# Low weight parts on GpSimd: one subtraction per row block instead of one per weight tile

## The chip, the cores and the metric

The kernel runs on one core of one Trainium2 chip. The metric is the device time of one execution in microseconds (us). Before the change three runs took 1737.58, 1738.07 and 1731.9 us; their median is 1737.58 us.

The engines are named as the profile names them: PE is the matrix engine and PEld its weight load, DVE the vector engine, ACT the scalar engine, POOL the GpSimd engine, and SP the queue that issues the kernel's DMAs. Each engine takes its own instructions in order. Where one needs another's result, it waits on a semaphore.

## What is computed

The reference is one inference step of a two-layer decoder trunk, for a prompt of 1024 tokens and 8 samples of 4 tokens (1056 columns in all), at model width 1024. Layer 0 is sliding-window attention, layer 1 a gated DeltaNet. Cut to what matters here:

```python
for layer in range(DEPTH):                      # DEPTH = 2
    hp, gp = modulate(xp, c_prompt, norm_g[layer], w_mod[layer], b_mod[layer])
    hs, gs = modulate(xs, c_sample, norm_g[layer], w_mod[layer], b_mod[layer])
    if layer % N_MIXERS == 0:
        op, kp, vp = swa_branch(hp, swa_w_in[j], swa_sinks[j], swa_w_out[j])
        ...
    else:
        op, cp, sp = gdn_branch(hp, conv0, s0, gdn_w_in[j], gdn_conv_w[j], ...)
        ...
    xp = xp + gp * op
    xs = xs + gs * osm
y_prompt = rms_norm(xp, final_norm_g)
```

Both branches begin with `h @ w_in`. In layer 0 `w_in` is 1024 x 2560, in layer 1 it is 1024 x 6176. Everything is float32. These input projections are the work that the change touches.

## The kernel before

**The products.** PE's fast float32 form (`fp32r`) keeps fewer bits than float32. So each operand is kept as a high part, which is the value rounded to that form, and a low part, which is what the rounding left. A product is the sum of three: high x high, high x low and low x high. For the activations these are `hhi`, `hlo` (layer 0) and `h2hi`, `h2lo` (layer 1), in eight row blocks of 128 rows of the model width. For the weights they are `wh` and `wl`.

**A weight tile.** A projection makes 128 output rows for all 1056 columns. Its weights, 1024 x 128, come in two halves. Each half is one tile of 128 partitions x 4 row blocks x 128 columns, loaded by `load_raw` (line 441) into one of four `wr` buffers. `split_w` (line 449) then makes the two parts: ACT casts the whole half into `wh` (line 456), and POOL subtracts that from the raw half into `wl` (line 457), 128 x 512 elements in one instruction. There are three `wh` and three `wl` buffers.

**Who calls it.** The first four halves (lines 716 and 722) and two more (line 749) belong to the opening part of layer 0, in which PE runs `first_half` (line 693) between the modulation's products. `vproj` (line 861) splits four tiles of 2 row blocks x 256 columns (`wvh`, `wvl`). `projector` (line 575) serves 15 projections of layer 0 and 47 of layer 1, two halves each. `first_weights` (line 1433) splits two halves for the first key projection of layer 1 (`kw0l`, `kw1l`), and `decays` (line 1522) two small tiles of 4 row blocks x 32 columns (`wab`).

**A projection in time.** `project` (line 548) walks the column groups 0:384, 384:768 and 768:1056. In each it walks the eight row blocks, with three matmuls for each: `wh` with the high activations, `wh` with the low ones, `wl` with the high ones. The eight row blocks of one group are eight ticks, a projection is 24 ticks. The first row block of the second half is needed at the fifth tick. While projection i runs, the job `ahead` (line 597) issues the loads of projection i+2 and the two splits of projection i+1, at ticks 2 and 20 (`SP`).

**What sets the order.** From line 1287 on, all instructions go through `Core`, a planner that runs while the program is written. `Core.issued` (line 111) charges each instruction a start and a length and keeps `free[engine]` and, for each tile, when it was written and last used. Between any two matmuls of a projection, `stages` (line 496) lets the waiting jobs (attention blocks, the DeltaNet's chains, gating, convolution taps, sample columns) issue what the planner holds to be ready: `ready`, `soon` and `idle` (lines 520 to 527) compare those times. `project` calls `until(ready(hi, lo))` at the first row block of each half, for the whole tiles `hi` and `lo`. The order found so is then fixed on every engine. The planner's charge on POOL is its element count per partition `n` by a rate and a fixed part:

```python
"gpsimd": (420, 0.02 if n >= 256 else 0.14)
```

An instruction that writes a tile which an instruction of the same engine last used starts at least 0.1 us after that one (`after`, line 161).

**What else POOL does.** In layer 1 it also computes the sample columns' convolution (`tp`, `us`, from `XS`), clears and fills the diagonal blocks of the triangular inverse (`UZ`, `Xd`, the latter from `Xc`, which a DMA brings), and computes the reciprocal square roots of the output norm (`rst`, `rsw`, `fo`; ACT scales `vo` with `fo`). DVE at the same time runs the convolution taps (`vT`, `kT`, `qT`), the decay blocks (`DP`) and the row-by-row inversion (`tmp`, `X`).

Of the kernel before, what the change touches and what calls it, by code (L numbers as in the profile page):

```python
# [191 lines left out]
def f(ap):  # L192
    return ap.bitcast(F32)
# [26 lines left out]
def body(tc, I, O, cst_ap, dbg=None):  # L220
    nc = tc.nc
# [227 lines left out]
    def split_w(raw, alloc=None):  # L449
        nk, ncol = raw.shape[1:]  # L450
        if alloc is None:
            hi = wq.tile([P, nk, ncol], F32R, tag="wh", name="wh", bufs=3)
            lo = wq.tile([P, nk, ncol], F32R, tag="wl", name="wl", bufs=3)
        else:
            hi, lo = alloc()
        last_split[:] = [nc.scalar.copy(hi, raw)]
        nc.gpsimd.tensor_sub(lo, raw, f(hi))
        return hi, lo

    def load_w(pieces, rows_ap, ncol, nk=4, alloc=None):  # L460

        return split_w(load_raw(pieces, rows_ap, ncol, nk), alloc)
# [112 lines left out]
    def projector(plan):  # L575
# [8 lines left out]
        def w_split(i, q):  # L584
            if i < len(plan):
                halves_.setdefault(i, []).append(split_w(raws[i][q]))
# [134 lines left out]
    with tc.issue_after(hi_.ins):  # L721
        fws[1] = [split_w(raw) for raw in raws]
# [39 lines left out]
    if True:  # L762
# [469 lines left out]
        for t in range(NB + 1):  # L1232
# [3 lines left out]
            for k in range(KD):  # L1236
                hi, lo = wv[k // 2]
# [49 lines left out]
        nc = Core(tc)  # L1287
# [23 lines left out]
    if True:  # L1311
# [124 lines left out]
        for i, t in enumerate(turned_):  # L1436
# [7 lines left out]
            for kk, hf in order if i < NB else sorted(order, key=lambda o: o[::-1]):  # L1444
                if True:
# [8 lines left out]
                    for k in range(4 * kk, 4 * kk + 4):  # L1454
# [3 lines left out]
                        hi, lo = whi[k][:, ns], wlo[k][:, ns]  # L1458
# [1221 lines left out]
    nc = nc.nc  # L2680
# [36 lines left out]
```

## Time and profile before

| | us |
|---|---|
| median of three runs | 1737.58 |
| profiled execution, its own time | 1730.22 |
| its span, first to last instruction | 1728.1 |
| PE busy | 1628.6 |
| PEld busy | 1432.1 |
| DVE busy | 1207.9 |
| ACT busy | 862.0 |
| POOL busy | 603.2 |

A row of a group of instructions gives: line, engine, operation, the tiles as out<-in, the shapes as partitions x elements, the count, then busy time in us, the mean of one in ns, and the idle time of the engine just before them with what ended it. Line 89 is the planner's recording call, so most instructions carry it, and the tile names tell them apart. A row of the view of stretches gives: the stretch and its length, then for each engine its busy time and (in brackets) its instructions, then the granted share of PE's clock, the DMA share and the DMA rate. A row of the timeline gives: start, length, engine, line, operation, tiles, shapes, count.

### The profile page before, as it was taken

How to read it: one execution, taken by the hardware profiler on the slowest of the kernel's cores; microseconds unless marked ns; L12 is line 12 of the kernel's file. 1: busy time of each engine (PE TensorE's matmuls, PEld its weight loads, DVE VectorE, ACT ScalarE, POOL GpSimd, SP SyncE). 2: the span in 40 equal slices, each digit the busy share in tenths (PEclk: the TensorE clock that was granted, in tenths of full speed). 3: DMA queues.
4: the chain of work that ended last, by engine and by line, in shares of the span. 5: the costliest groups of instructions: out<-in, count | busy, mean ns of one | idle time of the engine just before them, and what ended most of it. 6: DMA issues, size and time to landing. Idle time of an engine off the chain costs nothing. (4 is left out here: it accounts for less than half of the span.)

```text
span 1728.1 us, 31800 instructions
## 1 busy us (share of the span) xinstructions
PE 1628.6 (94%) x10666; PEld 1432.1 (83%) x10666; DVE 1207.9 (70%) x3538; ACT 862.0 (50%) x2514; POOL 603.2 (35%) x1170
## 2 busy tenths in 40 slices
PE   6999999998999899799999999999999998989897
PEld 5988888986777889689989999899998996667685
DVE  4526675564565678877887789778798876357677
ACT  4625555444334565256554665654756555332332
POOL 2601111112122334354443544545345454332322
PEclk9999999999999999899999999999999999999999
DMA  9542121233233232132412323224232137764785
GB/s 330 152 134 72 52 58 50 55 98 106 85 130 103 81 79 67 53 88 56 126 36 75 102 59 107 69 77 112 50 107 62 46 97 211 228 200 130 233 277 184
DMA packets 281573, 191.77 MB, mean 111 GB/s; under 512 B 98362, under 2 KB 253882, under 8 KB 281379
## 3 DMA queue, kind: packets, MB, share of 16 engines
q1 hardware_dynamic: 281410, 189.75, 38.1%
q8 instruction: 84, 1.38, 0.3%
q14 instruction: 79, 0.64, 0.1%
HBM read 144.68 MB, written 47.04 MB: 111 GB/s over the span
## 5 line engine op out<-in xcount | busy, mean ns | idle before, releaser
L89 PE MATMUL ps_pj<-h2hi,wl 128*128 128x384 f32 (+1 forms) x1128 | 380.4, 337 | 2.2 <-POOL wl L89 2.2
L89 PE MATMUL ps_pj<-h2hi,wh 128*128 128x384 f32 (+1 forms) x1128 | 378.3, 335 | 2.1 <-ACT wh L89 2.1
L89 PE MATMUL ps_pj<-h2lo,wh 128*128 128x384 f32 (+1 forms) x1128 | 379.4, 336 | 0.0
L89 POOL TENSOR_TENSOR wl<-wr,wh 128x512 fp32r<-128x512 f32 x122 | 164.4, 1348 | 517.5 <-ACT wh L89 432.9
L89 PEld LDWEIGHTS ps_pj<-h2hi,wl 128*128 128x128 f32 x1128 | 213.6, 189 | 6.2 <-POOL wl L89 3.1
L89 PEld LDWEIGHTS ps_pj<-h2hi,wh 128*128 128x128 f32 x1128 | 213.5, 189 | 4.3 <-ACT wh L89 2.4
L89 PEld LDWEIGHTS ps_pj<-h2lo,wh 128*128 128x128 f32 x1128 | 213.5, 189 | 3.2
L89 POOL TENSOR_TENSOR xt<-xt,y 128x512 f32<-128x512 f32 (+1 forms) x48 | 63.9, 1333 | 188.2 <-DVE y L89 165.1
L89 PE MATMUL ps_pj<-hlo,wh 128*128 128x384 f32 (+1 forms) x360 | 119.0, 331 | 0.0
L89 PE MATMUL ps_pj<-hhi,wh 128*128 128x384 f32 (+1 forms) x360 | 118.4, 329 | 0.0
L89 PE MATMUL ps_pj<-hhi,wl 128*128 128x384 f32 (+1 forms) x360 | 117.9, 328 | 0.0
L89 DVE SCALAR_TENSOR_TENSOR vT<-XR,cT,vT 128x384 f32<-128x384 f32 (+1 forms) x144 | 93.0, 658 | 29.0 <-ACT vT L89 27.1
L89 DVE TENSOR_TENSOR tmp<-X 64x31 f32<-64x31 f32 (+15 forms) x248 | 94.0, 379 | 10.4 <-POOL X L89 7.1
L89 DVE TENSOR_TENSOR X<-X,tmp 64x31 f32<-64x31 f32 (+15 forms) x248 | 94.6, 381 | 8.5
L89 ACT CAST wh<-wr 128x512 fp32r<-128x512 f32 x122 | 75.1, 616 | 16.4 <-PE ps_pj L89 12.0
L89 PEld LDWEIGHTS ps_pj<-hlo,wh 128*128 128x128 f32 x360 | 67.7, 188 | 11.2 <-issue 11.1
L89 ACT COPY XR<-ps_pj 128x384 f32<-128x384 f32 (+1 forms) x96 | 43.0, 448 | 55.9 <-PE ps_pj L89 55.7
L89 POOL TENSOR_TENSOR Xd<-Xc,cst 32x128 f32<-32x128 f32 x128 | 63.4, 495 | 21.2 <-DMA Xc<-Xdd 10.4
L89 PEld LDWEIGHTS ps_pj<-hhi,wh 128*128 128x128 f32 x360 | 67.7, 188 | 2.7 <-issue 2.7
L89 ACT ACTIVATE prob<-prob,nm 128x256 f32<-128x256 f32 (+1 forms) x128 | 62.2, 489 | 14.8 <-DVE nm L89 14.6
L89 PEld LDWEIGHTS ps_pj<-hhi,wl 128*128 128x128 f32 x360 | 67.7, 188 | 2.1 <-issue 2.1
L89 ACT ACTIVATE vo<-vo,fo 128x128 f32<-128x128 f32 x128 | 42.3, 392 | 54.0 <-POOL fo L89 54.0
(574 smaller groups left out, 4218.1 us busy)
## 6 DMA issues: line engine op xcount, KB each, us to landing
wr<-in_gdn_w_in SPq DMA_DIRECT2D x96, 256.0 KB
S<-in_state_gdn_s SPq DMA_DIRECT2D x40, 256.0 KB
xt<-in_x_prompt SPq DMA_DIRECT2D x16, 512.0 KB
wm<-in_w_mod SPq DMA_DIRECT2D x16, 512.0 KB
wr<-in_swa_w_in SPq DMA_DIRECT2D x64, 128.0 KB
wmod<-in_w_mod SPq DMA_DIRECT2D x32, 256.0 KB
wm<-in_w_mod SPq DMA_DIRECT2D x32, 256.0 KB
DP<-gcr SPq DMA_DIRECT2D x64, 128.0 KB
```

Source lines behind the costliest of these rows:

```text
L89: inst = fn(*args, **kwargs)
```

## The change

`split_w` issues the subtraction once for each row block: four instructions of 128 x 128 for a half tile, two of 128 x 256 for each of the four tiles of `vproj`, four of 128 x 32 for each of the two tiles of `decays`. The cast on ACT stays one instruction. What is computed is the same.

```diff
         last_split[:] = [nc.scalar.copy(hi, raw)]
-        nc.gpsimd.tensor_sub(lo, raw, f(hi))
+
+        for k in range(nk):
+            nc.gpsimd.tensor_sub(lo[:, k], raw[:, k], f(hi[:, k]))
         return hi, lo
```

## The prediction

> **What bounds the kernel now.** I read the page first, then the stretches, then what PE waited for, then the timeline around the subtractions.
>
> ```profile
> span 1728.1 us, 31800 instructions
> PE 1628.6 (94%) x10666; PEld 1432.1 (83%) x10666; DVE 1207.9 (70%) x3538; ACT 862.0 (50%) x2514; POOL 603.2 (35%) x1170
> ...
> L89 POOL TENSOR_TENSOR wl<-wr,wh 128x512 fp32r<-128x512 f32 x122 | 164.4, 1348 | 517.5 <-ACT wh L89 432.9
> ```
> ```profile
> 110.00:410.00 300.00, 293.48 (x2146) 255.18 (x2146) 188.49 (x691) 158.21 (x515) 42.63 (x36) 1.00 0.26 71
> 410.00:555.00 145.00, 137.72 (x690) 106.23 (x691) 77.78 (x236) 53.87 (x123) 34.80 (x30) 0.98 0.37 115
> 555.00:1000.00 445.00, 414.52 (x2859) 388.37 (x2857) 351.25 (x971) 240.98 (x718) 185.93 (x443) 0.98 0.29 75
> 1000.00:1443.00 443.00, 433.74 (x3083) 407.75 (x3083) 364.43 (x996) 258.58 (x821) 213.79 (x512) 1.00 0.31 83
> ```
>
> PE sets the time: it is busy in 94% of the span. From 110 to 1443 us, where nearly all of the changed subtractions lie, it is idle for 6.5 + 7.3 + 30.5 + 9.3 = 53.6 us (each stretch less its first busy time). POOL is half empty there (its busy time is the last one in the row), and it has idled 517.5 us ahead of the `wl` subtractions alone, nearly always for ACT's cast. DVE is second, at 80% in the last two rows.
>
> What PE loses to the low parts is small:
>
> ```profile
> PE ps_mi L89 <- DVE us L89: 6.7, 8, 1.6
> ...
> PE ps_lg L89 <- DVE UZ L89: 4.9, 7, 2.0
> ...
> PE ps_mi L89 <- DVE S L89: 3.5, 4, 2.1
> ...
> PE ps_pj L89 <- POOL wl L89: 2.2, 2, 1.5
> ```
> ```profile
> PEld ps_lg L89 <- POOL Xd L89: 5.2, 3, 2.3
> ...
> PEld ps_pj L89 <- POOL wl L89: 3.1, 3, 1.8
> ```
>
> The weight load waited three times for `wl`, 3.1 us together; the matmuls' 2.2 us are two of the same places.
>
> **The change part by part.** *POOL's own time.* There are 122 + 8 subtractions into `wl` and two into `kw0l`, `kw1l` that become four each. No 128 x 128 subtraction into `wl` exists in the trace, but the same operation on such a shape does, and a series with 128 elements on 32 partitions:
>
> ```profile
> L89 POOL TENSOR_TENSOR Xd<-Xc,cst 32x128 f32<-32x128 f32 x128 | 63.4, 495 | 21.2 <-DMA Xc<-Xdd 10.4 <-DVE UZ L89 2.0 <-ACT th L89 1.4
> ...
> L89 POOL TENSOR_TENSOR us<-us,tp 128x32 f32<-128x32 f32 x96 | 30.1, 313 | 8.0
> ...
> L89 POOL TENSOR_TENSOR wab<-wab,wab 128x128 fp32r<-128x128 f32 x2 | 0.9, 457 | 0.4 <-ACT wab L89 0.4
> ```
>
> Four at 457 ns are 1828 ns against 1348, so +0.48 us a half tile. The bounds: four at 450 ns (0.9 us busy for two) are +0.45, four at 495 ns (a mean that holds some disturbed ones) are +0.63. Over 132 halves that is 63 us more on POOL, 59 to 83. The two `wab` tiles go from one of 457 to four of 313 ns, +0.8 us each; the four `wvl` tiles only halve, between nothing and +0.48 each. All of this lies in POOL's idle time unless something is queued behind it. If nothing covered it, the price would be the whole 63 us.
>
> *What is queued behind it.* The samples' convolution, `Xd`, `UZ` and the chain of `rst` to `fo` sit behind a subtraction on POOL, and SP's load into the freed `wr` buffer waits for the subtraction, with other DMAs behind that load. The chain of work that ended last passes over a `wl` subtraction four times:
>
> ```profile
> 1038.56 1.83 POOL wl L89
> ...
> 1075.49 1.28 POOL wl L89
> 1077.27 3.22 DMA Xc<-Xdd
> ...
> 1256.56 1.30 POOL wl L89
> 1262.36 1.25 POOL wl L89
> ```
>
> At 1075.49 it is just this case: the `Xc` transfer left SP's queue after `wl` was done, and `Xd` then waits for it. I charge the four steps of the chain, 4 x 0.48 = +1.9 us. The lower bound is nothing, since another chain of almost the same length may take over; the upper bound is treated with the rivals.
>
> *The head start.* The first row block is finished after 0.46 us instead of 1.35. One of the three stalls shows what that is worth:
>
> ```profile
> 857.07 0.34 PE L89 MATMUL ps_pj<-h2lo,wh 128*128 128x384 f32 x1
> 858.90 0.45 PE L89 MATMUL ps_pj<-h2hi,wl 128*128 128x384 f32 x1 [1.50 <-POOL wl L89]
> ```
> ```profile
> 857.43 0.20 POOL L89 TENSOR_TENSOR fo<-rst,rsw 128x4 f32<-128x4 f32 x1
> 857.58 1.27 POOL L89 TENSOR_TENSOR wl<-wr,wh 128x512 fp32r<-128x512 f32 x1
> ```
>
> The subtraction stood behind the chain to `fo`, and the first matmul on `wl` began 0.05 us after its end. With pieces it could begin at about 858.1, 0.8 us earlier. It then uses one row block every three matmuls, and POOL makes one every 0.46 us, so the later pieces keep up:
>
> ```profile
> 911.24 0.34 PE L89 MATMUL ps_pj<-h2lo,wh 128*128 128x384 f32 x1
> 911.41 0.34 PE L89 MATMUL ps_pj<-h2hi,wl 128*128 128x384 f32 x1
> 911.59 0.34 PE L89 MATMUL ps_pj<-h2hi,wh 128*128 128x384 f32 x1
> ```
>
> Matmuls start 0.17 us apart, three in 0.52 us. Three stalls at up to 0.89 us give −2.7 us; the bounds are 0 and −3.1, for a stall can't give more than it has. That PE waits for pieces singly shows in the opening part, where it read block 2 of `hlo` while POOL was still writing block 3 of the same tile:
>
> ```profile
> 48.88 0.34 PE L702 MATMUL ps_pj<-hlo,wh 128*128 128x384 f32 x1
> ```
> ```profile
> 46.81 2.59 POOL L675 TENSOR_TENSOR hlo<-fu,hhi 128x1024 fp32r<-128x1024 f32 x1 [0.73 <-ACT hhi L674]
> ```
>
> *PE's added waits.* Three more matmuls of each half wait on POOL. Where the wait was long fulfilled, as at 911.41 (the first use of a half whose subtraction, below, ended at 909.16), the matmuls keep their 0.17 us, so I charge nothing; 10 ns on each of some 390 would be 3.9 us, my upper bound.
>
> ```profile
> 907.87 1.29 POOL L89 TENSOR_TENSOR wl<-wr,wh 128x512 fp32r<-128x512 f32 x1 [6.07 <-ACT wh L89]
> ```
>
> *DVE beside POOL.* While a subtraction runs, some DVE operations stretch:
>
> ```profile
> 1036.66 0.37 DVE L89 TENSOR_TENSOR X<-X,tmp 64x207 f32<-64x207 f32 x1
> ...
> 1039.16 1.48 DVE L89 TENSOR_TENSOR tmp<-X 64x231 f32<-64x231 f32 x1
> ```
> ```profile
> 697.59 0.51 DVE L89 TENSOR_TENSOR tmp<-X 64x192 f32<-64x192 f32 x1
> ```
> ```profile
> 695.71 2.72 POOL L89 TENSOR_TENSOR Xd<-Xc,cst 32x128 f32<-32x128 f32 x5
> ```
>
> Alone such an operation takes 0.37 us; beside the `wl` of 1038.56 it took 1.48; beside a series of short POOL instructions, which is what the change makes, 0.51, one after another, while POOL kept a pace of 0.54. A dense series would cost DVE 4 x 0.14 = 0.56 us a half against 1.1 at once. DVE's gain is then up to half a us for each half that meets such operations, up to 132 x 0.55 = 73 us of DVE time if all did; POOL's longer stay eats some of it. DVE does not bound: the three rows of PE's waits for it above hold 15.1 us. I take −1 us, with bounds of −15 and +5 (the same 15.1 grown by POOL's 0.48/1.35).
>
> The Trainium skill says in "SBUF — State Buffer", section "Who interferes with whom", that GpSimd and a DVE instruction with two SBUF inputs share a read port as an exclusive lock, held for the whole instruction, so that the second fully blocks. The rows of 1038.56 and 1039.16 agree with it, 1.48 us against 0.37. By that rule alone the longest block falls from one 1.3 us instruction to one piece of 0.46.
>
> *The planner.* It charged a half 0.02 + 512/420 = 1.24 us. Now it charges 4 x (0.14 + 128/420) + 3 x 0.1 = 2.08 us, because each piece writes the tile that the one before it wrote. So `lo` is ready 0.84 us later in the plan, POOL's jobs shift, and the woven order of all engines changes from the first planned split on. No row prices this. It can win part of PE's 53.6 us of idle time, at most half of it I think, or lose as much. A matmul of a projection behind foreign work shows 0.45 instead of 0.34 us (858.90), so a hundred more such interruptions would be +11 us. I take +2 us, for the planner now holds back the second half and fills the place with jobs that interrupt.
>
> *The sum.* +1.9 − 2.7 + 0 − 1 + 2 = +0.2 us on the profiled execution's 1730.22 (span 1728.1 and 2.1 around it), 1730.4. The runs' median is 7.4 us above that execution; put on the median, 1737.58 + 0.2 gives 1738.
>
> **The rivals.** *POOL's queue comes onto the path (slower).* The place is layer 1 from 555 to 1443 us, where 92 halves are split (45 and 47, the instructions of the last engine in these rows of the `wl` tiles alone) and POOL is busy 42 and 48%.
>
> ```profile
> 555.00:1000.00 445.00, 184.47 (x546) 103.96 (x546) 61.99 (x45) 0.98 0.29 75
> 1000.00:1443.00 443.00, 195.44 (x581) 109.43 (x581) 63.40 (x47) 1.00 0.31 83
> ```
>
> The price is 92 x 0.48 = 44 us of delay to `Xd`, `fo`, the samples and the loads behind them. For it speak the chain's four `wl` steps and the 5.2 us for `Xd`; against it the small share of PE's waits that name POOL. It decides once more than some 20 of the 92 reach PE (9.6 us). With a third of them: +15 us, 1752.
>
> *DVE is freed (faster).* If DVE's blocked time is what holds the DeltaNet's chain, the 92 halves save up to 0.5 us each, 46 us of DVE time; with a third reaching PE, −15 us, 1722. For it speak DVE's 80% and the long stretches; against it that PE's waits for DVE are 15.1 us in these rows, so it needs nearly all of them. The Trainium skill's lock, named above, is the rule by which it would come out so.
>
> *The pieces don't start PE earlier (the change doesn't do what it says).* If the tile were released as a whole, the head start is gone and `wl` comes 0.48 us later at the three stalls: +2.7 + 1.4 on the forecast, 1742. The `hlo` rows speak against it.
>
> **How the numbers follow.** A measurement of this kernel can tell about 0.5%, 8.7 us, from no change, so that is the line between the classes. The forecast has a chance of 0.37 and the whole-tile case 0.06; both are within 8.7 us of 1737.58, together 0.43. POOL's queue, with a planner's order that loses, has 0.32, the freed DVE with an order that wins 0.25. The range goes from the freed DVE's 1722 to some way past POOL's queue at 1752, to 1757, for half of 44 us would be 1760. The forecast's own range, by its terms' bounds without the planner's, is 1737.58 − 3.1 − 15 to 1737.58 + 1.9 + 3.9 + 5, which is 1719 to 1748.
>
> **What would show it.** Right: four `wl` instructions of about 0.46 us for each half, POOL near 667 us; PE's waits for `wl` under 1 us; DVE's longest `tmp` and `vT` well under 1.4 us; PE's busy time within a few us of 1628.6. Wrong: PE idle with `Xd`, `vo` or `Xc` as what ended it, or DVE busy much under 1180 us with a shorter span. If instead PE's busy time grows by more than 5 us at the same matmul count, the new order costs through interruptions, and my +2 was too small.

## The result and the profile after

The changed kernel takes 1736.84 us (median of 12 runs, 1732.34 to 1740.54), the kernel before 1735.96 us (12 runs). The ratio is 1.0007 with a 95% interval of 0.9993 to 1.0022: no difference that can be measured, as predicted. All ratios here compare undisturbed executions with those of the kernel before in the same batch, so a ratio can differ a little from the quotient of two medians, and two executions of *e11* in a slower state (1824.29 and 2263.79 us) count in its median alone. The profiled execution behind the rows below took 1732.34 us. From its page, first the span and the engines, then PE's busy share in slices and two groups:

```profile
span 1730.6 us, 32224 instructions
...
PE 1621.2 (94%) x10666; PEld 1429.5 (83%) x10666; DVE 1174.6 (68%) x3538; ACT 862.6 (50%) x2514; POOL 675.5 (39%) x1576
...
PE   6999999999999999589999999999999998989897
...
L89 POOL TENSOR_TENSOR wl<-wr,wh 128x128 fp32r<-128x128 f32 x488 | 236.7, 515 | 485.5 <-ACT wh L89 449.4
...
L89 PEld LDWEIGHTS ps_pj<-h2hi,wl 128*128 128x128 f32 x1128 | 213.2, 189 | 2.7 <-POOL wl L89 0.2
```

POOL's time rose by 72.3 us, DVE's fell by 33.3, PE's by 7.4, and the weight load now waits 0.2 us for `wl` instead of 3.1. All of that should help, yet the span is 2.5 us longer. So PE's idle time grew by 9.9 us, and the slices show where: the 5 is new (a 7 before). The same two stretches as before, on the changed kernel:

```profile
555.00:1000.00 445.00, 406.01 (x2827) 380.34 (x2826) 334.81 (x956) 236.51 (x715) 211.09 (x578) 0.97 0.29 75
1000.00:1443.00 443.00, 433.13 (x3080) 410.69 (x3079) 351.36 (x995) 257.14 (x814) 240.76 (x653) 1.00 0.30 82
```

The first lost 8.5 us of PE's busy time against 414.52. What PE waited for:

```profile
PE ps_lg L89 <- DVE UZ L89: 19.0, 6, 16.9
```

One wait of 16.9 us holds nearly all of these 19.0. The timeline of DVE's queue, then of PE:

```profile
681.20 0.69 DVE L89 STREAM_TRANSPOSE UZ<-Xd 128x512 f32<-128x512 f32 x1
681.83 0.17 DVE L89 TENSOR_TENSOR tmp<-X 64x60 f32<-64x60 f32 x1
...
706.31 0.18 DVE L89 TENSOR_TENSOR X<-X,tmp 64x31 f32<-64x31 f32 x1
706.42 0.60 DVE L89 SCALAR_TENSOR_TENSOR DP<-ps_lg,sj,DP 128x128 f32<-128x128 f32 x2
706.94 0.69 DVE L89 STREAM_TRANSPOSE UZ<-Xd 128x512 f32<-128x512 f32 x1
```
```profile
708.01 1.06 PE L89 MATMUL ps_lg<-UZ,M 128*32 128x64 f32 x16 [16.92 <-DVE UZ L89]
```

Between two transposes stand 60 instructions of the inversion (`tmp`, `X`) of the next head. The planner had put them there because each pair is let go when its clock holds DVE idle. On the chip they take 25 us, and an earlier head's transpose, for which PE waits, stands behind them. The wait costs more than its length: PE's granted clock was 1.00 from 680 to 691 us, 0.52 from 708 to 717 us, behind the wait, and 1.00 again from 717 to 730 us. PE was busy for 8.48 us of that middle stretch, so about 4 us more are lost there (an estimate: half of that time). The long series is in the new order, not in the pieces as such, and the experiments separate the two.

### The profile page after: what moved, and what is told of

It reads as the page before. It is cut to its first block, busy times and chain, and to the rows that moved or that the text cites. A ratio compares the mean times of both kernels' runs of the same rounds, so it can differ in the third digit from the quotient of the medians.

```text
span 1730.6 us, 32224 instructions
## 1 busy us (share of the span) xinstructions
PE 1621.2 (94%) x10666; PEld 1429.5 (83%) x10666; DVE 1174.6 (68%) x3538; ACT 862.6 (50%) x2514; POOL 675.5 (39%) x1576
## 5 line engine op out<-in xcount | busy, mean ns | idle before, releaser
L89 POOL TENSOR_TENSOR wl<-wr,wh 128x128 fp32r<-128x128 f32 x488 | 236.7, 515 | 485.5 <-ACT wh L89 449.4
L89 DVE SCALAR_TENSOR_TENSOR vT<-XR,cT,vT 128x384 f32<-128x384 f32 (+1 forms) x144 | 83.9, 591 | 47.4 <-ACT vT L89 45.3
L89 DVE TENSOR_TENSOR tmp<-X 64x31 f32<-64x31 f32 (+15 forms) x248 | 89.0, 359 | 16.9 <-POOL X L89 13.4
L89 DVE TENSOR_TENSOR X<-X,tmp 64x31 f32<-64x31 f32 (+15 forms) x248 | 90.7, 366 | 8.5
L89 ACT CAST wh<-wr 128x512 fp32r<-128x512 f32 x122 | 75.1, 617 | 16.4 <-PE ps_pj L89 11.3
L89 ACT ACTIVATE qe<-ps_mi,Eg 128x128 f32<-128x128 f32 x112 | 34.9, 363 | 60.4 <-PE ps_mi L89 60.3
```

The costliest lines, as they stand in the source:

```text
L89: inst = fn(*args, **kwargs)
```

## The experiments

**How order and form were taken apart.** The change does two things: POOL gets four instructions, and the planner, charging them more, weaves all engines into another order. In the experiments the planner's record of a half (in *e2*, its four records) is chosen apart from how many instructions go to POOL. A longer charge gives a new order. With the same charge PE, ACT, DVE and SP have the same instructions in the same order, whole or in pieces; the traces of each such pair agree in it, instruction by instruction. The four orders: that of before (charge as before), the changed one (+0.84 us a half), a third (+0.60) and a fourth (+0.30).

*e1*: pieces in the order of before (the loop stands inside one record):

```diff
-        nc.gpsimd.tensor_sub(lo, raw, f(hi))
+        nc.in_pieces(lo, raw, f(hi), 1)
+    def in_pieces(self, lo, raw, hi, step):
...
+        for k in range(0, nk, step):
...
+            inst = self.nc.gpsimd.tensor_sub(lo[:, ks], raw[:, ks], hi[:, ks])
...
+        self.issued("gpsimd", "tensor_sub", inst.ins, (lo, raw, hi), {})
```

> The order of before on every engine, the low part in four pieces on POOL; the planner charges it as one instruction. Theory (the pieces help on the chip, and the new order lost that at one place, a PE idle time of 16.9 us at 691 to 708 us): PE's waits for wl fall from 3.1 us to under 1 us, DVE busy from 1208 to about 1175 us as in the changed kernel, no PE idle time above 5 us between 110 and 1443 us, and a time of 1722 to 1732 us beside 1736 of before. Rival 1 (the pieces do nothing for PE; only the order differs, and two orders of one kernel lie about equal): within 2 us of before, with DVE's busy time down all the same. Rival 2 (the pieces cost, the order wins it back): slower by 3 us or more.

Measured: 1737.62 us against 1734.63, ratio 1.0017 (1.0000 to 1.0034). The expected gain didn't come. Alone, the pieces cost some 3 us (0 to 6 by the interval), just at the edge of what can be told from nothing. From its page:

```profile
span 1739.4 us, 32230 instructions
...
PE 1631.4 (94%) x10666; PEld 1435.9 (83%) x10666; DVE 1172.4 (67%) x3538; ACT 860.9 (49%) x2514; POOL 681.6 (39%) x1576
```

DVE gave back 35.5 us here too. Instruction by instruction, PE falls behind the kernel before most at two places. The first, on ACT and on PE, in pieces:

```profile
640.74 0.23 ACT L89 ACTIVATE us<-us 128x32 f32<-128x32 f32 x1 [5.65 <-POOL us L89]
```
```profile
647.66 0.90 PE L89 MATMUL ps_tr<-cst,vT 128*128 128x128 f32 x3 [7.79 <-ACT vT L89]
```

and the same instructions in the kernel before:

```profile
635.74 0.23 ACT L89 ACTIVATE us<-us 128x32 f32<-128x32 f32 x1 [1.10 <-POOL us L89]
```
```profile
642.67 0.55 PE L89 MATMUL ps_tr<-cst,vT 128*128 128x128 f32 x3 [3.69 <-ACT vT L89]
```

POOL's sample sums `us` come later. One of the two halves that lie ahead of them and among them, in pieces and before:

```profile
633.71 2.27 POOL L159 TENSOR_TENSOR wl<-wr,wh 128x128 fp32r<-128x128 f32 x4
```
```profile
630.80 1.28 POOL L89 TENSOR_TENSOR wl<-wr,wh 128x512 fp32r<-128x512 f32 x1
```

The other took 2.89 us against 2.33. From the first of the two halves to the last `us` POOL needs 11.3 us rather than 8.0. The pieces' own length is 1.55 us of that; the rest is in POOL's small instructions between them (the first `us` took 1.15 us, not 0.48). POOL also came to these halves 1.2 us later, beside ACT. ACT waits 4.5 us longer for `us`, and everything behind it on ACT, `vT` among it, comes 5 us later to PE. The second place has the chain to `fo` behind a subtraction, in pieces:

```profile
1263.29 2.33 POOL L159 TENSOR_TENSOR wl<-wr,wh 128x128 fp32r<-128x128 f32 x4
...
1269.39 0.20 POOL L89 TENSOR_TENSOR fo<-rst,rsw 128x4 f32<-128x4 f32 x1
```
```profile
1269.62 0.98 ACT L89 ACTIVATE vo<-vo,fo 128x128 f32<-128x128 f32 x3 [6.93 <-POOL fo L89]
1270.51 0.35 ACT L89 COPY uo<-ps_ob 128x256 f32<-128x256 f32 x1
```
```profile
1270.92 1.22 PE L89 MATMUL ps_mi<-uo,DP 128*128 128x128 f32 x4 [3.38 <-ACT uo L89]
```

and before:

```profile
1261.77 0.99 ACT L89 ACTIVATE vo<-vo,fo 128x128 f32<-128x128 f32 x3 [4.36 <-POOL fo L89]
```
```profile
1263.07 0.71 PE L89 MATMUL ps_mi<-uo,DP 128*128 128x128 f32 x4 [0.98 <-ACT uo L89]
```

PE waits 4.1 and 2.4 us longer at the two places. The copy of `uo` needs nothing from POOL; it only stands behind `vo` on ACT. Not all of the second delay is the pieces: from `wl` to `fo` POOL took 1.1 us longer, and it came to `wl` later by 1.5, having waited 6.82 us for the transfer into `X` rather than 5.34. Behind both waits PE is slower as well, as the rows show: three matmuls in 0.90 us, not 0.55, and four in 1.22, not 0.71. Its granted clock was 0.50 from 647.6 to 653 us, where the kernel before had 1.00 (642.6 to 647).

*e2*: one instruction in the changed order (planner charged for four):

```diff
-        nc.gpsimd.tensor_sub(lo, raw, f(hi))
+        nc.as_pieces(nc.nc.gpsimd.tensor_sub(lo, raw, f(hi)), lo, raw, f(hi))
+    def as_pieces(self, inst, lo, raw, hi):
+        for k in range(raw.shape[1]):
+            self.issued("gpsimd", "tensor_sub", inst.ins, (lo[:, k], raw[:, k], hi[:, k]), {})
```

> The order of the changed kernel on every engine, the low part as one instruction on POOL; the planner charges it as four. Theory: the PE idle time near 700 us stays at about 17 us, the waits for wl and DVE's long stretches come back (DVE busy about 1208 us), so 1741 to 1752 us. Rival 1: within 2 us of the changed kernel's 1737. Rival 2: 1733 or less.

Measured: 1746.5 us, ratio 1.0071 (1.0045 to 1.0097), as its theory had it. The order alone costs about 12 us, and the long wait is there without any pieces. Its page and its wait:

```profile
PE 1624.6 (93%) x10666; PEld 1429.9 (82%) x10666; DVE 1208.7 (69%) x3538; ACT 862.8 (50%) x2514; POOL 595.5 (34%) x1170
```
```profile
PE ps_lg L89 <- DVE UZ L89: 19.8, 9, 16.8
```

The changed kernel is this one with pieces, and it is 1.0007 / 1.0071 = 0.9936 of it (about 0.991 to 0.997, the half widths added in squares): in this order the pieces save some 11 us.

*e3*: two pieces of 256 columns, order of before (`in_pieces` with a step of 2):

> The order of before, the low part in two pieces of 256 columns on POOL. If the gain of pieces is that DVE is blocked for a shorter time and that PE can start early: DVE busy between the whole and the quarters, about 1190 us, POOL about 625 us, and a time between before and the run with four pieces. Rival (the pieces do nothing): within 2 us of before.

Measured: 1734.44 us, ratio 1.0002 (0.9987 to 1.0016). Nothing lost and nothing won, as the rival had it. PE's waits at the two places of *e1* lie in between (5.44 and 2.85 us), and so does DVE:

```profile
PE 1625.8 (94%) x10666; PEld 1430.3 (83%) x10666; DVE 1195.6 (69%) x3538; ACT 861.6 (50%) x2514; POOL 636.2 (37%) x1304
```

**What the subtraction costs at all.** *e4*: in its place POOL fills the tile with zeros, in the order of before. (SP's order of issue isn't quite kept in some runs: here, in *e5* and in *e9* it differs from before at 51 to 56 of 1119 places, in *e10* at 133, in *e11* from *e6* at 112. PE, ACT and DVE keep theirs.)

```diff
-        nc.gpsimd.tensor_sub(lo, raw, f(hi))
+        nc.cleared(lo, raw, f(hi))
...
+    def cleared(self, lo, raw, hi):
+        inst = self.nc.gpsimd.memset(f(lo), 0.0)
+        self.issued("gpsimd", "tensor_sub", inst.ins, (lo, raw, hi), {})
```

> The low part of the weights is left out: POOL only clears the tile, which reads nothing, about 0.5 us a half; order of before otherwise. It shows the most that POOL's subtractions can cost. Theory: DVE is not stretched by them, so DVE busy is 1208 less some 60 to 75 us, PE never waits for wl, and the time is at or below that of four pieces, 1715 to 1730 us. Rival 1 (DVE's blocked time and the wl waits don't matter to PE): within 3 us of before.

Measured: 1708.32 us, ratio 0.985 (0.9823 to 0.9878), below even the theory's range. This takes away 26 us, but three things at once: POOL's time, its reading beside DVE, and the wait for the cast. The next two runs give POOL's time back (*e5*), then the wait as well (*e9*).

```diff
+        for n in range(3):
             inst = self.nc.gpsimd.memset(f(lo), 0.0)
```

> Order of before on every engine; in place of the subtraction POOL fills the tile with zeros three times, reading nothing (the low part of the weights is left out). One such fill of 128 x 512 took about 0.53 us, so three are about 1.6 us, a little longer than the one subtraction. What is told apart is why the single fill saved 26 us. Theory 1, reading beside DVE is what the subtraction costs (DVE's instructions stretch): DVE busy stays near 1138 us, and the time near 1710 us. Theory 2, POOL's time is what it costs (the queue behind it, and the wait for the tile): DVE may be short, but the time comes back to 1735 us or above. Between the two, say 1722 us, each has half.

Measured: 1713.64 us against 1735.46, ratio 0.9871 (0.9847 to 0.9894), with DVE busy 1142.7 us: near theory 1.

```diff
+            if n == 0:
+                self.tc.add_manual_dep(inst.ins, cast.ins.name, ...)   # a semaphore wait
```

> As e5 (order of before, three fills of the tile with zeros in place of the subtraction; the low part of the weights is left out), but the first fill of a half waits for ACT's cast, as the subtraction does, wherever its tile is free already. e5 came to 1713.64 us, 22 us under before, and its fills could start before the cast. Theory 1, the reading beside DVE is the cost: again 1711 to 1718 us. Theory 2, e5 won by starting early (no queue behind a wait for the cast, the tile ready sooner): 1728 to 1738 us.

Measured: 1717.45 us against 1734.63, ratio 0.9892 (0.9866 to 0.9919), again as theory 1 had it. Its page:

```profile
span 1712.6 us, 32008 instructions
...
PE 1622.2 (95%) x10666; PEld 1431.7 (84%) x10666; DVE 1147.5 (67%) x3538; ACT 859.9 (50%) x2514; POOL 629.5 (37%) x1446
...
L89 PE MATMUL ps_pj<-h2hi,wl 128*128 128x384 f32 (+1 forms) x1128 | 380.4, 337 | 2.8 <-POOL wl L157 2.8
L157 POOL MEMSET wl<- 128x512 f32 x366 | 193.7, 530 | 510.7 <-ACT wh L89 472.2
```

POOL works longer on `wl` than before (193.7 us against 164.4) and still waits for the cast, but it reads nothing, and 0.0108 x 1735 = 18.7 us are gone (14 to 23 by the interval) with 60.4 us of DVE's time. That the tile holds zeros does not make PE faster: its matmuls on `wl` took 337 ns, as before. One tile's view (count, then shortest, median and longest in ns) shows it on `vT`, first before, then in this run, then in the changed kernel:

```profile
L89 DVE SCALAR_TENSOR_TENSOR vT<-XR,cT,vT x144: 468/609/1730, 636.4 to 1410.6; 128x384 f32<-128x384 f32 x96, 128x256 f32<-128x256 f32 x48
```
```profile
L89 DVE SCALAR_TENSOR_TENSOR vT<-XR,cT,vT x144: 469/610/643, 633.3 to 1395.9; 128x384 f32<-128x384 f32 x96, 128x256 f32<-128x256 f32 x48
```
```profile
L89 DVE SCALAR_TENSOR_TENSOR vT<-XR,cT,vT x144: 464/610/892, 627.6 to 1412.1; 128x384 f32<-128x384 f32 x96, 128x256 f32<-128x256 f32 x48
```

The median is the same. The longest falls from 1730 ns to 892 with pieces and to 643 with fills. Of the 26 us of *e4*, POOL's time and the wait for the cast bring back some 7 together (the intervals of neighbouring runs overlap), and 19 stay gone. So reading beside DVE is most of what the subtraction costs, by elimination. Three other things differ in this run and weren't taken apart: the `wr` buffer is free as soon as the cast is done, POOL's instruction may itself be held up less, and SP issues its loads a little differently.

**Two more orders.** The charge is set in the planner's table:

```diff
-                           "gpsimd": (420, 0.02 if n >= 256 else 0.14)}[eng]
+                           "gpsimd": (420, 0.62 if op == "split" else 0.02 if n >= 256 else 0.14)}[eng]
```

with the record named `split` (0.62 for the third order, 0.32 for the fourth). *e6*: four pieces in the third order.

> Four pieces, with the planner charging 0.60 us more for a half (1.84 us, about what four pieces of 0.46 us take on the chip) instead of 0.84 more: a third order, in which DVE's queue has no 60 instructions of the inversion in one piece (the longest series in it is 10). Theory 1, the 17 us stall is what the changed order costs: without it the pieces are at 1736 - 15 = 1721 us, faster than both. Theory 2, an order that was not searched for is worse by about 12 us in many small places, of which the pieces give 10 back: 1733 to 1745 us, with no long stall.

Measured: 1725.51 us against 1735.46, ratio 0.9949 (0.9929 to 0.9969), nearer theory 1. *e7*: one instruction in that order.

> The third order, one instruction a half. Theory 1, the pieces save about 10 us wherever PE isn't held elsewhere (e2 against the changed kernel): this run is 10 us above the third order in pieces, with DVE busy 25 to 35 us more. Theory 2, what the pieces give hangs on the order (in the order of before they lost 3 us): the two runs differ by less than 5 us, or the other way.

Measured: 1724.47 us, ratio 0.9949 (0.9932 to 0.9966), so theory 2: the gain is the order's. The engines in pieces, then whole:

```profile
PE 1630.2 (95%) x10666; PEld 1433.8 (83%) x10666; DVE 1168.5 (68%) x3538; ACT 862.4 (50%) x2514; POOL 683.7 (40%) x1576
```
```profile
PE 1629.1 (95%) x10666; PEld 1431.2 (83%) x10666; DVE 1200.8 (70%) x3538; ACT 862.4 (50%) x2514; POOL 599.4 (35%) x1170
```

Both beat the kernel before by about 9 us (0.0051 x 1735), and DVE's 32.3 us and POOL's 84.3 between them move nothing. *e8*: four pieces in the fourth order.

> Four pieces, with the planner charging 0.30 us more for a half: a fourth order, in which DVE's longest series of the inversion is 10 instructions. Theory 1, only an order with the long series is bad: about 1722 to 1730 us. Theory 2, orders scatter by about 10 us either way whatever the planner was told: anything from 1725 to 1750 us, not in the order of the charges 0, 0.30, 0.60, 0.84.

Measured: 1745.3 us against 1735.46, ratio 1.0062 (1.0040 to 1.0084), without any long wait of the kind seen in the changed order: theory 2. So a long series on DVE is not what makes an order bad in general. *e12*: one instruction in that order.

> The fourth order (1745.3 us in pieces) with one instruction a half. The pieces were worth +3 us (slower) in the order of before, -10 in the changed one and +1 in the third. Theory 1, their worth hangs on the order and is within 10 us either way: 1735 to 1755 us. Theory 2, they help wherever the order is a bad one: 1752 to 1758 us.

Measured: 1747.58 us against 1734.63, ratio 1.0072 (1.0047 to 1.0098): theory 1. This order loses otherwise than the changed one. In its profile PE's busy time is 1645.9 us, 17.3 us over that of before, which is most of the 22.6 us by which the span is longer, and the mean granted clock is 0.976 against 0.983. All eight:

| order (charge) | one instruction | four pieces | pieces / one |
|---|---|---|---|
| of before (0) | 1 | 1.0017 | 1.0017 |
| fourth (+0.30) | 1.0072 | 1.0062 | 0.9990 |
| third (+0.60) | 0.9949 | 0.9949 | 1.0000 |
| changed (+0.84) | 1.0071 | 1.0007 | 0.9936 |

The orders lie 1.2% apart (21 us) and don't follow the charge. The pieces are worth something certain in one of the four; the half widths of the last column are 0.002 to 0.0035.

**Letting the followers go first.** *e10*, in the order of before: each of the last three pieces is sent behind the next POOL instruction, at the latest before PE's first use of the tile:

```diff
+    def in_pieces(self, lo, raw, hi):
...
+        self.pending = [(lo[:, k], raw[:, k], hi[:, k]) for k in range(1, raw.shape[1])]
...
             self.core.issued(self.name, op, inst.ins, args, kwargs)
+            if self.name == "gpsimd":
+                self.core.piece()
```

> Order of before on PE, ACT and DVE; four pieces, but each of the last three is sent behind the next instruction of POOL instead of ahead of it (at the latest before PE's first matmul on the tile). So an instruction that follows waits for one piece of 0.5 us, not for four. Theory 1, what made e1 (1737.62 us) lose against the order of before is POOL's queue ahead of fo and the samples: the two jumps of 4.1 and 2.4 us go, and the time is 1725 to 1733 us. Theory 2, the pieces lose by something else (more instructions, or DVE's blocked time spread wider): 1735 to 1741 us as e1.

Measured: 1751.4 us against 1734.63, ratio 1.0084 (1.0055 to 1.0112). Both theories missed: it is 1.0084 / 1.0017, some 12 us, above the pieces in a row. POOL's and PE's timeline:

```profile
1424.94 0.72 POOL L174 TENSOR_TENSOR wl<-wr,wh 128x128 fp32r<-128x128 f32 x1 [3.59 <-ACT wh L93]
1430.09 0.20 POOL L93 TENSOR_TENSOR rst<-rsw 128x4 f32<-128x4 f32 x1 [4.43 <-DVE rsw L93]
1430.24 0.45 POOL L164 TENSOR_TENSOR wl<-wr,wh 128x128 fp32r<-128x128 f32 x1
```
```profile
1430.75 0.44 PE L93 MATMUL ps_pj<-h2hi,wl 128*128 128x384 f32 x1 [1.34 <-POOL wl L164]
```

The second piece could have run at once, but stood behind a follower that waited 4.43 us for DVE, and PE came to the piece first. *e11*, the same in the third order:

> The third order with the interleaved pieces of e10. Theory 1, POOL's queue eats what the pieces give in that order too (1725.51 us in pieces, 1724.47 us whole): 1716 to 1722 us, the fastest of all. Theory 2: 1723 to 1728 us, no difference.

Measured: 1739.29 us against 1734.63, ratio 1.001 (0.9987 to 1.0034), 1.001 / 0.9949 or some 11 us above that order with pieces in a row. Neither theory holds here either. In these rows ready work was put behind work that wasn't. They don't account for 12 and 11 us: all of PE's waits for `wl` are 4.5 us in *e10* and 1.3 in *e11*, and SP's order differs in both. Why the interleaved pieces lose stays open.

## Why the prediction was right, and where it wasn't

The time (1738 against 1736.84) and the class came out by luck. The sum gave the pieces 1.9 − 2.7 − 1 = −1.8 us and the planner +2, and the runs show neither. With one instruction a half the new order costs 12 us, and the pieces in it save 11. Taken the other way round, the pieces in the order of before cost some 3 us, and the new order with pieces is then worth −2 (1.0007 / 1.0017), which can't be told from nothing. The two effects don't add, as the sum took for granted.

- *POOL's time.* 0.457 us for a piece was taken from two `wab` instructions; 488 pieces took 515 ns on the mean, and POOL came to 675.5 us, not 667. The upper bound, 495 ns, was too low. An undisturbed piece was priced right: in the order of before their median is 462 ns. The mean is above it since some pieces stretch: four took 1.71 us at 863.35 (below) and 2.33 at 1263.29 (above).
- *Head start.* Right in mechanism. In the order of before the first matmul on the piece at the 858.90 place waited 0.43 us rather than 1.50:

```profile
863.35 1.71 POOL L159 TENSOR_TENSOR wl<-wr,wh 128x128 fp32r<-128x128 f32 x4
```
```profile
863.86 0.44 PE L89 MATMUL ps_pj<-h2hi,wl 128*128 128x384 f32 x1 [0.43 <-POOL wl L159]
```

  The matmul started 0.5 us after the series of four began, not after its end. PE read a piece while the next was being made, so the case of the whole tile released at once is out.
- *PE's added waits, taken as nothing.* In the order of before the matmuls on `wl` went from 337 to 339 ns, and those on `wh` with the high part, which have no such wait, from 335 to 337. The added waits can't be told from nothing.

```profile
L89 PE MATMUL ps_pj<-h2hi,wl 128*128 128x384 f32 (+1 forms) x1128 | 381.9, 339 | 0.4 <-POOL wl L159 0.4
...
L89 PE MATMUL ps_pj<-h2hi,wh 128*128 128x384 f32 (+1 forms) x1128 | 379.7, 337 | 2.1 <-ACT wh L89 2.1
```

- *DVE beside POOL, −1 us.* The step that failed is "DVE does not bound: the three rows of PE's waits for it above hold 15.1 us". These are three of seventeen rows that name DVE in that view of the kernel before, and all of them hold 38.1 us. The four largest of the others:

```profile
PE ps_lg L89 <- DVE KQT L89: 4.4, 1, 4.4
...
PE ps_lg L89 <- DVE gpr L89: 3.2, 1, 3.2
PE ps_pj L650 <- DVE dg L638: 2.8, 1, 2.8
PE ps_ob L89 <- DVE vo L89: 2.4, 5, 0.6
```

  So 15.1 us was no bound on what a freer DVE can give: with POOL's reads away (*e9*) 18.7 us were won, though by more than the pieces free. In that profile PE idles 9.1 us less and is busy 6.4 us less than before. The waits that name DVE fall to 31.5 us (leaving out one of 9.7 us that the view of before puts down to a DMA), those for POOL's `Xd` from 4.2 us to none. What the pieces' share of it is worth by itself, no run shows. The exclusive lock of the Trainium skill ("SBUF — State Buffer", section "Who interferes with whom") agrees with the longest `vT` of 1730 and 892 ns: each began within 0.02 us of a `wl` instruction, of 1300 ns (at 1221.72 us before) and of 458 ns (at 800.87 us in the changed kernel), and each ended 0.41 us after it. Beside fills, which read nothing, no `vT` took over 643 ns.
- *POOL's queue, +1.9 us.* Mis-sized: at two places of the order of before alone PE waits 4.1 + 2.4 us longer, in part for the pieces' length. It was also put on POOL's own chain, and it came by ACT's queue, through instructions that don't need POOL.
- *The planner, +2 us.* Mis-sized by a factor of six with one instruction a half (with pieces the order is worth about nothing), and with the reason wrong: "the planner now holds back the second half and fills the place with jobs that interrupt". PE's busy time fell by 4.0 us in the changed order as one instruction (1624.6 against 1628.6); it idled instead, 16.8 us of it at one place. The 0.45 us that priced an interruption is no such row: that matmul stands behind a wait of 1.50 us. Other charges gave −9 and +12 us, and in the one of +12 PE's busy time did grow. The forecast that PE's busy time stays within a few us fell with it: it was 7.4 us lower in the changed kernel. The other signs came: PE's matmuls don't wait for `wl`, the weight load waits 0.2 us, and DVE's longest `vT` took 892 ns.

Of the rivals, POOL's queue and the freed DVE both show in the runs, at opposite signs, and neither alone decides. Why do the pieces save 11 us in one order and lose some 3 in another, when DVE gets back 30 to 36 us in each? In the order of before the two delayed places show where part of the gain goes. In the changed order the gain is spread over many places, and what makes it larger there than in the third was not settled; nor was the rest of the loss in the order of before beyond those 6.5 us and the slower clock behind them.

## What to carry to other kernels

When a kernel's order comes from a planner, any edit that changes a charge is two edits; run the new order with the old instruction and the new instruction in the old order before crediting either. Here the order alone was worth −0.5 to +0.7%, about as much as the edit under test at its best, and the versions that beat both kernels are those with a charge of 0.60 us more, in pieces or not (1724.47 us with one instruction). And a bound that is read from a view of waits needs all of its rows: three rows of 15.1 us stood here for seventeen of 38.1. Even the whole sum can miss a delay that passes through another engine's queue; in *e1* the late POOL reached PE as waits for ACT.

## What the runs showed of the hardware beyond expectation

A POOL instruction that only writes hardly disturbs DVE: 366 fills of 530 ns left the longest `vT` at 643 ns against a median of 610, where subtractions of 1348 ns had stretched one to 1730. And cutting a subtraction in four divides the longest block but removes only some six tenths of what the fills remove: DVE's time fell by 35.5 us with pieces, by 60.4 with fills. And a long wait of PE costs more than its length: behind waits of 7.8 and 16.9 us the granted clock was 0.50 and 0.52 for the next 5 and 9 us.
